# Prompt attention with both key heads side by side: scores in two PSUM banks at once, value products alternating between column halves

## The chip, the core and the metric

The kernel runs on one core of one Trainium2 chip. The metric is the device time of one execution in microseconds (us), a median of three runs. A profile of one more execution lists what each engine did: PE is TensorE (PEld its weight loads), DVE VectorE, ACT ScalarE, POOL GpSimd, SP the queue that issues most DMAs.

## What is computed

One inference step of a hybrid decoder with two layers, for a prompt of 512 tokens and for 8 sample sequences of 8 tokens that share the weights. Each layer has a token-mixing half (attention, convolution, retention and gated DeltaNet from one input projection, merged with gates) and a channel-mixing half. The change lies in the attention of the token-mixing half: 4 query heads in 2 groups over 2 key heads of 64 channels. For each block of 128 prompt queries, with the causal mask in the bias:

```
s = jnp.einsum('bqkgd,bnkd->bkgqn', qb, kb[:, :, 0]).astype(jnp.float32) + jnp.transpose(rb[t5_bucket(dist)], (2, 3, 0, 1))
p = masked_softmax(s, mask)
return jnp.einsum('bkgqn,bnkd->bqkgd', p.astype(dt), kb[:, :, 1])
...
o = g[:, :, 0] * o_c + g[:, :, 1] * o_s + g[:, :, 2] * o_w
```

There are three branches: compressed blocks (`o_c`), selected blocks (`o_s`, at this length all of them) and the sliding window (`o_w`). The sample sequences also need scores of their 8 query rows against 2048 cached keys, which lie in pages of the cache.

## The kernel before

The program is traced in Python and put in order by a list scheduler with its own estimates of time. What runs on the chip is a fixed order per engine; each engine works through its own and waits on semaphores. Pools give out tiles: a tag with `bufs=n` has n slots, and a new tile of that tag waits until the old one in its slot has been read.

`nsa` runs `nsa_prompt` and `sample_scores` in turns, a piece of the one and a piece of the other. Beside them the scheduler puts the products of the merges (`mm`, lines 335 to 337: 128x288 in fp32r, three per 128 channels), which depend on neither and serve as filling for PE; those that find no place here follow later. All other products here are plain fp32, and each is two PE instructions in the trace.

`nsa_prompt` first makes the compressed keys and values and that branch's probabilities, then goes over 4 query blocks i (with i+1 key blocks of 128 each), 2 groups g, 2 key heads kv and 2 branches br (selected, window). One unit (i, g, kv, br) is a chain over four engines:

- PE, L1551: scores of 128 queries against n = i+1 key blocks, contraction over 64 channels (rows 0-63 or 64-127 of the array, by the key head), into one bank of tag `s`.
- DVE L1553 adds the bias, L1555 takes the negated maximum; ACT L1557 makes the exponentials `E` with their sum; DVE L1558 and L1560 divide and apply the gate.
- PE L1563 transposes E by blocks into the single bank `t`; ACT (the helper on L603) copies it to `ET`.
- PE L1567: n value products into 64 of the 128 partitions of bank `o`, by the key head. L1546 puts the product of the compressed branch there before.

`sample_scores` loads pages by indirect DMAs on POOL (L1421, two of 128 KB for each `pg` tile, 8 tiles in all) and multiplies them on PE (L1590). One of its 8 units per layer takes 4 `pg` tiles, so that the other 4 can be loading. Its results lie in one bank of `s` and in bank `ax` of another pool; after every second unit ACT copies both out.

PSUM has 8 banks: 3 for `mm`, 1 for `ax`, and in this phase 2 for `s`, 1 for `t`, 1 for `o`.

## Time and profile before

| | us |
|---|---|
| median of 3 runs | 2760.32 |
| the runs | 2750.40, 2761.28, 2760.32 |
| span of the profiled execution | 2759.1 |
| stretch of the prompt attention, layer 0 (577 to 733 us) | 156 |
| the same, layer 1 (1934 to 2090 us) | 156 |

The span is what the profile shows of one execution, from the first to the last instruction; the page gives no other time of that execution. PE is busy for 94% of the span. The two stretches begin at the first score product of a layer and end with the last products on the sample's cached keys.

### The profile page before, as it was taken

The numbers are of one execution on the slowest core, as the hardware profiler recorded it, in microseconds if no ns is written. First come the engines' busy times: TensorE is split into PE (matmuls) and PEld (weight loads), VectorE is DVE, ScalarE is ACT, GpSimd is POOL, SyncE is SP. The second block draws the span as 40 slices with busy tenths as digits, with TensorE's granted clock in tenths as the row PEclk, the third lists the DMA queues.
The fourth block names the chain that finished last, engine by engine and source line by source line (L and its number), as shares of the span: only waits on it lengthen the run. The fifth ranks groups of instructions, "written<-read, shape, count | busy, mean of one in ns | idle before, by whom it ended". The sixth has DMA issues, their size and how long they took to land. (4 is left out here: it accounts for less than half of the span.)

```text
span 2759.1 us, 54028 instructions
## 1 busy us (share of the span) xinstructions
PE 2600.8 (94%) x22658; PEld 2275.4 (82%) x22658; DVE 1412.4 (51%) x2892; ACT 933.2 (34%) x1777; POOL 635.0 (23%) x827
## 2 busy tenths in 40 slices
PE   6999999988989999999989999999889999999998
PEld 4768777866779999999987687788657899999997
DVE  5878533333534573435578784432336155634455
ACT  4315112322323453323452342222233244433233
POOL 2102321223352320101122022212334333101012
PEclk9999989998999999999999999989799999999999
DMA  8643344322353242332466324413224451423324
GB/s 304 208 171 119 131 139 177 108 88 70 112 161 100 95 130 85 128 101 84 127 217 225 117 92 136 151 55 123 62 77 147 126 168 42 125 84 127 101 81 133
DMA packets 125058, 346.74 MB, mean 126 GB/s; under 512 B 28076, under 2 KB 47536, under 8 KB 118608
## 3 DMA queue, kind: packets, MB, share of 16 engines
q1 hardware_dynamic: 104016, 275.05, 30.6%
q0 software_dynamic: 20800, 68.25, 7.9%
q8 instruction: 178, 2.92, 0.4%
q14 instruction: 64, 0.52, 0.1%
HBM read 330.77 MB, written 20.73 MB: 127 GB/s over the span
## 5 line engine op out<-in xcount | busy, mean ns | idle before, releaser
L335 PE MATMUL mm<-hh,whi 128*128 128x288 f32 x3136 | 959.4, 306 | 8.8 <-ACT whi L287 4.1
L337 PE MATMUL mm<-hh,wlo 128*128 128x288 f32 x3136 | 948.8, 303 | 5.7 <-DVE wlo L288 4.2
L336 PE MATMUL mm<-hl,whi 128*128 128x288 f32 x3136 | 951.5, 304 | 2.5 <-issue 2.5
L288 DVE TENSOR_TENSOR wlo<-raw,whi 128x1024 fp32r<-128x1024 f32 (+1 forms) x320 | 391.6, 1226 | 577.5 <-ACT whi L287 538.3
L335 PEld LDWEIGHTS mm<-hh,whi 128*128 128x128 f32 x3136 | 602.8, 192 | 40.5 <-issue 22.7
L336 PEld LDWEIGHTS mm<-hl,whi 128*128 128x128 f32 x3136 | 606.2, 193 | 24.5 <-issue 20.9
L337 PEld LDWEIGHTS mm<-hh,wlo 128*128 128x128 f32 x3136 | 603.3, 192 | 23.2 <-issue 15.1
L287 ACT ACTIVATE whi<-raw 128x1024 fp32r<-128x1024 f32 (+1 forms) x320 | 334.9, 1048 | 562.0 <-PE mm L336 328.4
L337 PE MATMUL mm<-acth,wlo 128*128 128x288 f32 x704 | 206.4, 295 | 2.0 <-DVE wlo L288 2.0
L335 PE MATMUL mm<-acth,whi 128*128 128x288 f32 x704 | 208.2, 296 | 0.1
L336 PE MATMUL mm<-actl,whi 128*128 128x288 f32 x704 | 207.7, 296 | 0.0
L558 POOL COPY nfp<-gb 128x2 f32<-128x2 f32 x44 | 42.4, 964 | 611.8 <-ACT gb L532 611.8
L1421 POOL DMA_INDIRECT pg<-ck,ix x128 | 125.8, 983 | 183.6 <-PE sc L1590 89.5
L1786 POOL TENSOR_TENSOR f<-f,gate 128x288 f32<-128x288 f32 x80 | 77.1, 974 | 319.3 <-DVE gate L1785 316.2
L337 PEld LDWEIGHTS mm<-acth,wlo 128*128 128x128 f32 x704 | 131.9, 188 | 2.6 <-DVE wlo L288 2.5
L336 PEld LDWEIGHTS mm<-actl,whi 128*128 128x128 f32 x704 | 132.9, 189 | 0.8 <-DVE actl L344 0.5
L335 PEld LDWEIGHTS mm<-acth,whi 128*128 128x128 f32 x704 | 132.2, 188 | 1.2 <-ACT acth L343 1.0
L1421 POOL DMA_INDIRECT fil<-cc,ix x64 | 69.1, 1079 | 178.6 <-PE cmps L1462 165.0
L697 DVE SCALAR_TENSOR_TENSOR cvy<-cgb,par,cvy 128x512 f32<-128x512 f32 x120 | 91.8, 782 | 0.0
L1785 DVE SCALAR_TENSOR_TENSOR gate<-gate,mm 128x288 f32<-128x288 f32 x80 | 35.8, 450 | 101.6 <-PE mm L337 92.4
L1764 ACT ACTIVATE gate<-mm 128x288 f32<-128x288 f32 x112 | 45.2, 403 | 122.4 <-PE mm L337 103.4
L1553 DVE TENSOR_TENSOR s<-s,nb 128x256 f32<-128x256 f32 (+1 forms) x64 | 25.5, 398 | 118.4 <-PE s L1551 96.0
(585 smaller groups left out, 4262.0 us busy)
## 6 DMA issues: line engine op xcount, KB each, us to landing
raw<-wtr SPq DMA_DIRECT2D x124, 512.0 KB
raw<-wup SPq DMA_DIRECT2D x104, 512.0 KB
f<-wada SPq DMA_DIRECT2D x32, 1024.0 KB
fil<-wada SPq DMA_DIRECT2D x16, 1024.0 KB
raw<-wdn SPq DMA_DIRECT2D x32, 512.0 KB
raw<-wdn SPq DMA_DIRECT2D x32, 448.0 KB
raw<-wbr SPq DMA_DIRECT2D x16, 512.0 KB
raw<-wout SPq DMA_DIRECT2D x16, 512.0 KB
```

The lines of the kernel that those rows point to most:

```text
L287: nc.scalar.activation(hi, raw, AF.Copy)
L288: nc.vector.tensor_sub(lo, raw, hi.bitcast(F32))
L335: nc.tensor.matmul(ps, hi[:, k0 + k], ah[:, s], start=first, stop=False)
L336: nc.tensor.matmul(ps, hi[:, k0 + k], al[:, s], start=False, stop=False)
L337: nc.tensor.matmul(ps, lo[:, k0 + k], ah[:, s], start=False, stop=last)
L558: nc.gpsimd.tensor_copy(newp[:, ft], g[:, SEQ:SEQ + 2])
L697: nc.vector.scalar_tensor_tensor(y[:, :SEQ], gb[:, j:j + SEQ], wj(j), y[:, :SEQ], op0=OP.mult, op1=OP.add)
L1421: self.nc.gpsimd.indirect_dma_start(out=dst, out_offset=None, in_=self.ap[src], in_offset=bass.IndirectOffsetOnAxis(ap=ix[:, l, b, j:j + 1 ...
L1553: nc.vector.tensor_add(S[:, lo:], S[:, lo:], nb[:, hd, (0 if i else P):])
L1764: self.nc.scalar.activation(gts[hf], ps, AF.Tanh, scale=0.5)
L1785: nc.vector.scalar_tensor_tensor(gm, gm, 1.0, ps, op0=OP.add, op1=OP.mult)
L1786: nc.gpsimd.tensor_add(fm, fm, gm)
```

## The change

The loop over key heads moves inside the loop over branches. For each (i, g, br):

- one tile `s2` of two banks (a single slot) replaces the two slots of `s`; the scores of both key heads are written one behind the other, each into its own bank and from its own half of the array's rows;
- the steps on DVE and ACT are the same, for one head after the other; both `E` and both `ET` slots are taken by the two heads of one pair;
- the value products of the two heads alternate, block by block, between partitions 0-63 and 64-127 of `o`. A new helper, `in_one_go`, keeps all of them behind the first, which needs the `ET` that is ready last;
- the two products of the compressed branch stand side by side.

`sample_scores` takes two units at once: 8 `pg` tiles (16 indirect DMAs) are loaded, then all products run in one go, those on the last loaded tiles first. Its results, and the few products at the start of `nsa_prompt`, use bank `t` in place of `s`. The rest of the diff takes out comments and docstrings.

```diff
+    @contextmanager
+    def in_one_go(self):
+
+        info = mybir.DependencyInfo(mybir.DependencyClass.NoSync, mybir.DependencyReason.SCHED_ONLY)
+        ins = self.nc.cur_bb.bb.instructions
+        n = len(ins)
+        yield
+        first, *rest = [i for i in self.nc.cur_bb.bb.instructions[n:] if isinstance(i, mybir.InstMatmult)]
+        for i in rest:
+            self.tc.add_manual_dep(i, first.name, info, reason="in one go")
...
-        ps = self.ps("s", 2)
+        ps = self.ps("t")
...
+        rows = [slice(64 * kv, 64 * kv + 64) for kv in range(2)]
         for i in range(4):
             s = slice(i * P, (i + 1) * P)
             nk = (i + 1) * P
+            lo = max(0, i - 1) * P
             for g in range(2):
                 po = self.ps("o")
-                for kv in range(2):
-                    b = 64 * kv
+                for kv, r in enumerate(rows):
                     hd = 2 * kv + g
-                    nc.tensor.matmul(po[b:b + 64, :P], vc[32 * hd:32 * hd + 32, b:b + 64], PcT[32 * hd:32 * hd + 32, s],
-                                     start=True, stop=False, tile_position=(32 * hd, b))
-                    for br in range(2):
-                        ps = self.ps("s", 2)
-                        S = ps[:, :nk]
-                        nc.tensor.matmul(S, q[g][b:b + 64, s], kT[br][b:b + 64, :nk], start=True, stop=True)
-                        lo = max(0, i - 1) * P
-                        nc.vector.tensor_add(S[:, lo:], S[:, lo:], nb[:, hd, (0 if i else P):])
+                    nc.tensor.matmul(po[r, :P], vc[32 * hd:32 * hd + 32, r], PcT[32 * hd:32 * hd + 32, s],
+                                     start=True, stop=False, tile_position=(32 * hd, 64 * kv))
+                for br in range(2):
+                    S = self.cps.tile([P, 2, 512], F32, tag="s2", name="s2", bufs=1)
+                    for kv, r in enumerate(rows):
+                        nc.tensor.matmul(S[:, kv, :nk], q[g][r, s], kT[br][r, :nk], start=True, stop=True)
+                    E = []
+                    for kv in range(2):
+                        hd = 2 * kv + g
+                        nc.vector.tensor_add(S[:, kv, lo:nk], S[:, kv, lo:nk], nb[:, hd, (0 if i else P):])
                         nm, ss = self.pt("nm", (1,), bufs=4), self.pt("ss", (1,), bufs=4)
-                        nc.vector.tensor_reduce(nm, S, AX.X, OP.max, negate=True)
-                        E = self.pt("E", (SEQ,), bufs=2)
-                        nc.scalar.activation(E[:, :nk], S, AF.Exp, bias=nm, accum_out=ss)
+                        nc.vector.tensor_reduce(nm, S[:, kv, :nk], AX.X, OP.max, negate=True)
+                        e = self.pt("E", (SEQ,), bufs=2)
+                        nc.scalar.activation(e[:, :nk], S[:, kv, :nk], AF.Exp, bias=nm, accum_out=ss)
                         nc.vector.reciprocal(ss, ss)
                         gc = gt[:, i, 4 * (br + 1) + hd:4 * (br + 1) + hd + 1]
-                        nc.vector.tensor_scalar(E[:, :nk], E[:, :nk], ss, gc, op0=OP.mult, op1=OP.mult)
+                        nc.vector.tensor_scalar(e[:, :nk], e[:, :nk], ss, gc, op0=OP.mult, op1=OP.mult)
+                        E.append(e)
+                    ET = []
+                    for kv in range(2):
                         pt = self.ps("t")
                         for j in range(i + 1):
-                            nc.tensor.transpose(pt[:, j * P:(j + 1) * P], E[:, j * P:(j + 1) * P], self.ident)
-                        ET = self.pt("ET", (SEQ,), bufs=2)
-                        self.evac(ET[:, :nk], pt[:, :nk])
+                            nc.tensor.transpose(pt[:, j * P:(j + 1) * P], E[kv][:, j * P:(j + 1) * P], self.ident)
+                        et = self.pt("ET", (SEQ,), bufs=2)
+                        self.evac(et[:, :nk], pt[:, :nk])
+                        ET.append(et)
+                    with self.in_one_go():
                         for j in range(i + 1):
-                            nc.tensor.matmul(po[b:b + 64, :P], kvb[j][:, P * br + b:P * br + b + 64], ET[:, j * P:(j + 1) * P],
-                                             start=False, stop=br == 1 and j == i)
+                            for kv, r in reversed(list(enumerate(rows))):
+                                nc.tensor.matmul(po[r, :P], kvb[j][:, P * br + 64 * kv:P * br + 64 * kv + 64],
+                                                 ET[kv][:, j * P:(j + 1) * P], start=False, stop=br == 1 and j == i)
                 self.evac(o[g][:, s], po[:, :P])
                 yield
     def sample_scores(self, l, qd, Ss):
-        nc = self.nc
-        for G, i in ((0, 0), (0, 1), (0, 2), (0, 3), (1, 0), (1, 1), (1, 2), (1, 3)):
+        nc = self.nc
+        for G, i in ((0, 0), (0, 2), (1, 0), (1, 2)):
             big = []
-            for b4 in range(4):
-                pg = self.page_tile().rearrange("p (i a n) -> p i a n", i=2, a=2)
-                for t in range(2):
-                    self.pages(pg[:, t].rearrange("p a n -> p (a n)"), "ck", self.ix2, l, 4 * G + b4, 2 * i + t)
-                big.append(pg)
+            for u in range(2):
+                for b4 in range(4):
+                    pg = self.page_tile().rearrange("p (i a n) -> p i a n", i=2, a=2)
+                    for t in range(2):
+                        self.pages(pg[:, t].rearrange("p a n -> p (a n)"), "ck", self.ix2, l, 4 * G + b4, 2 * (i + u) + t)
+                    big.append(pg)
             yield
-            if i % 2 == 0:
-                sc = [self.ps("s", 2), self.ax("sc1")]
-            t = i % 2 * 2
-            with self.after_pe():
-                for kv in range(2):
-                    for b4 in range(4):
-                        for e in range(2):
-                            nc.tensor.matmul(sc[e][32 * b4:32 * b4 + 32, t * P:(t + 2) * P],
-                                             qd[64 * e:64 * e + 64, kv, 4 * G + b4].rearrange("p a g t -> p (a g t)"),
-                                             big[b4][64 * e:64 * e + 64, :, kv], start=kv == 0, stop=kv == 1,
-                                             tile_position=(64 * e, 32 * b4))
-            if t:
-                for e in range(2):
-                    self.evac(Ss[G][:, :PAST].rearrange("p (t e n) -> p t e n", e=2, n=P)[:, 2 * i - 2:2 * i + 2, e],
-                              sc[e].rearrange("p (t n) -> p t n", n=P))
+            yield
+            sc = [self.ps("t"), self.ax("sc1")]
+            with self.in_one_go():
+                for u in (1, 0):
+                    for kv in range(2):
+                        for b4 in (3, 2, 1, 0):
+                            for e in range(2):
+                                nc.tensor.matmul(sc[e][32 * b4:32 * b4 + 32, 2 * u * P:(2 * u + 2) * P],
+                                                 qd[64 * e:64 * e + 64, kv, 4 * G + b4].rearrange("p a g t -> p (a g t)"),
+                                                 big[4 * u + b4][64 * e:64 * e + 64, :, kv], start=kv == 0, stop=kv == 1,
+                                                 tile_position=(64 * e, 32 * b4))
+            for e in range(2):
+                self.evac(Ss[G][:, :PAST].rearrange("p (t e n) -> p t e n", e=2, n=P)[:, 2 * i:2 * i + 4, e],
+                          sc[e].rearrange("p (t n) -> p t n", n=P))
```

The number of instructions on each engine does not change (18413 on PE by the built program, where a product of two passes is one). Only their order does. Below, rows of the built order, without times; line numbers of the changed program are its own (L1564 scores, L1581 transposes, L1588 values, L1559 compressed branch, L1612 sample scores, L346 to L348 `mm`, L1432 page loads, L1807 the addition to `f`).

PE, second query block (i = 1), first group, layer 0. Before, each head's product stands alone:

```order
L1546 MATMUL o<-PcT,vc 64x128
L1551 MATMUL s<-kwin,nq 128x256
L1563 MATMUL t<-cst,E 128x128 x2
L1551 MATMUL s<-ksel,nq 128x256
L337 MATMUL mm<-bh,wlo 128x288
L1567 MATMUL o<-ET,kvb_6066 64x128
L1567 MATMUL o<-ET,kvb_6094 64x128
L335 MATMUL mm<-bh,whi 128x288
```

The same place now:

```order
L1559 MATMUL o<-PcT,vc 64x128 x2
L1581 MATMUL t<-cst,E 128x128 x2
L1564 MATMUL s_6505<-kwin,nq 128x256 x2
L1581 MATMUL t<-cst,E 128x128 x2
L346 MATMUL mm<-hh,whi 128x288
L347 MATMUL mm<-hl,whi 128x288
L348 MATMUL mm<-hh,wlo 128x288
L346 MATMUL mm<-hh,whi 128x288
L1588 MATMUL o<-ET,kvb_6066 64x128 x2
L1588 MATMUL o<-ET,kvb_6094 64x128 x2
```

Scores, values and compressed products of the two heads now stand in twos. This holds for all 16 value groups and all 8 compressed pairs of a layer, and for 10 of the 16 score pairs. In the other 6, all with i = 2 or 3, the scheduler puts the transposes of the pair before between the two scores.

PE, third query block (i = 2), layer 0, before:

```order
L1551 MATMUL s<-kwin,nq 128x384
L337 MATMUL mm<-hh,wlo 128x288
L335 MATMUL mm<-hh,whi 128x288
L1563 MATMUL t<-cst,E 128x128 x3
L336 MATMUL mm<-hl,whi 128x288
L337 MATMUL mm<-hh,wlo 128x288
L335 MATMUL mm<-hh,whi 128x288
L336 MATMUL mm<-hl,whi 128x288
L337 MATMUL mm<-hh,wlo 128x288
L1567 MATMUL o<-ET,kvb_6066 64x128
L1567 MATMUL o<-ET,kvb_6094 64x128
L1567 MATMUL o<-ET,kvb_6122 64x128
```

and now, at the same query block, a split pair:

```order
L1581 MATMUL t<-cst,E 128x128 x3
L1564 MATMUL s_6709<-kwin,nq 128x384
L1581 MATMUL t<-cst,E 128x128 x3
L1564 MATMUL s_6709<-kwin,nq 128x384
L1588 MATMUL o<-ET,kvb_6066 64x128 x2
L1588 MATMUL o<-ET,kvb_6094 64x128 x2
L1588 MATMUL o<-ET,kvb_6122 64x128 x2
```

There the second score of a pair moves behind the transposes of the pair before and directly ahead of that pair's values.

POOL, layer 0, from the start of the attention on, before (the row of 16 is two units of 8, and the second 8 wait for the products of a unit):

```order
L1530 MEMSET Pc 128x512
L1786 TENSOR_TENSOR f<-f,gate 128x288 x2
L1421 DMA pg<-ck,ix_158 128x256 x16
L1786 TENSOR_TENSOR f<-f,gate 128x288 x2
L1421 DMA pg<-ck,ix_158 128x256 x8
```

and now:

```order
L1541 MEMSET Pc 128x512
L1807 TENSOR_TENSOR f<-f,gate 128x288 x4
L1432 DMA pg<-ck,ix_158 128x256 x16
L1807 TENSOR_TENSOR f<-f,gate 128x288 x2
L1432 DMA pg<-ck,ix_158 128x256 x16
```

Page loads that were released 8 at a time are released 16 at a time, three times within the stretch where there were six releases.

## Rows read from the trace of the kernel before

**Rows 1.** The page: busy time, share of the span, instructions of each engine.

```profile
PE 2600.8 (94%) x22658; PEld 2275.4 (82%) x22658; DVE 1412.4 (51%) x2892; ACT 933.2 (34%) x1777; POOL 635.0 (23%) x827
```

**Rows 2.** Windows: length, busy us (instructions) by engine, granted clock, DMA share, GB/s.

```profile
577.00:733.00 156.00, 134.44 (x914) 95.38 (x914) 61.38 (x150) 49.32 (x130) 55.40 (x60) 0.88 0.23 70
...
1934.00:2090.00 156.00, 137.40 (x917) 96.20 (x916) 61.82 (x150) 49.65 (x131) 55.45 (x60) 0.87 0.23 70
```

**Rows 3.** Groups by form, 577 to 733: count | busy, mean ns | idle before.

```profile
L1567 PE MATMUL o<-ET,kvb 128*64 128x128 f32 x160 | 28.2, 314 | 16.5 <-ACT ET L603 13.2 <-issue 3.2
...
L1553 DVE TENSOR_TENSOR s<-s,nb 128x256 f32<-128x256 f32 x24 | 10.3, 431 | 47.8 <-PE s L1551 41.7 <-remote 3.1 <-PE o L1546 1.6
...
L1555 DVE TENSOR_REDUCE nm<-s 128x1 f32<-128x512 f32 x8 | 5.5, 690 | 0.2
L1557 ACT ACTIVATE E<-s,nm 128x512 f32<-128x512 f32 x8 | 5.5, 686 | 5.5 <-DVE nm L1555 5.5
```

**Rows 4.** Timeline of PE: start, duration in us, line, names, shapes, [idle before].

```profile
671.20 0.30 PE L335 MATMUL mm<-bh,whi 128*128 128x288 f32 x1
671.42 0.91 PE L1551 MATMUL s<-kwin,nq 64*128 64x384 f32 x2
672.26 0.55 PE L1563 MATMUL t<-cst,E 128*128 128x128 f32 x3
...
672.78 0.29 PE L337 MATMUL mm<-bh,wlo 128*128 128x288 f32 x1
...
673.18 0.29 PE L337 MATMUL mm<-bh,wlo 128*128 128x288 f32 x1
673.45 0.87 PE L1567 MATMUL o<-ET,kvb 128*64 128x128 f32 x6
674.25 0.40 PE L335 MATMUL mm<-bh,whi 128*128 128x288 f32 x1
674.49 0.30 PE L336 MATMUL mm<-bl,whi 128*128 128x288 f32 x1
```

**Rows 5.** Timeline of PE where two heads' scores happen to be neighbours.

```profile
695.18 0.69 PE L1551 MATMUL s<-kwin,nq 64*128 64x512 f32 x1
695.18 0.69 PE L1551 MATMUL s<-ksel,nq 64*128 64x512 f32 x1
...
696.24 1.09 PE L1567 MATMUL o<-ET,kvb 128*64 128x128 f32 x8
```

**Rows 6.** Timeline of PE from sample scores to compressed product to scores.

```profile
667.03 0.40 PE L1590 MATMUL s<-pg,qd 64*32 64x256 f32 x1
...
668.06 0.43 PE L1546 MATMUL o<-PcT,vc 32*64 32x128 f32 x2
668.41 0.59 PE L1551 MATMUL s<-ksel,nq 64*128 64x384 f32 x1
```

**Rows 7.** Timeline of PE in the sample's values: products on four column tiles.

```profile
791.21 1.06 PE L1731 MATMUL o<-pg,pT 128*32 128x128 f32 x26
792.20 0.49 PE L1728 MATMUL o<-nvx,cT 128*128 128x128 f32 x2
```

**Rows 8.** Timeline of PE around one of its long waits.

```profile
658.60 0.29 PE L336 MATMUL mm<-hl,whi 128*128 128x288 f32 x1
662.77 1.45 PE L1567 MATMUL o<-ET,kvb 128*64 128x128 f32 x6 [3.88 <-ACT ET L603]
```

**Rows 9.** Timeline of ACT at the same place.

```profile
662.23 0.49 ACT L603 ACTIVATE ET<-t 128x384 f32<-128x384 f32 x1 [3.94 <-remote]
```

**Rows 10.** Timeline of POOL, first and last of the 8 page loads there.

```profile
650.60 1.16 POOL L1421 DMA_INDIRECT pg<-ck,ix  x1 [3.45 <-PE sc L1590]
...
659.60 0.95 POOL L1421 DMA_INDIRECT pg<-ck,ix  x1 [0.30 <-issue]
```

**Rows 11.** Windows around the 14 page loads from 508 to 527, earlier in layer 0.

```profile
515.00:535.00 20.00, 16.79 (x87) 14.84 (x87) 4.38 (x16) 2.18 (x5) 9.18 (x11) 0.74 0.48 144
535.00:545.00 10.00, 10.00 (x86) 10.00 (x85) 1.33 (x2) 2.50 (x5) 0.00 (x0) 1.00 0.40 115
```

More of the change, by code (lines that the diff above doesn't have):

```diff
@@ L1488, in nsa_prompt @@
             nc.vector.tensor_scalar(kc[b:b + 64, b // 8:b // 8 + 8], ps[b:b + 64, :8], pc[b:b + 64], None, op0=OP.add)
-        ps = self.ps("s", 2)
+        ps = self.ps("t")
         for hd in range(4):
@@ L1507, in nsa_prompt @@
         Sc = self.pt("Sc", (4, 4, 8))
-        ps = self.ps("s", 2)
+        ps = self.ps("t")
         for g in range(2):
@@ L1512, in nsa_prompt @@
         self.evac(ST, ps[:64])
-        ps = self.ps("s", 2)
+        ps = self.ps("t")
         for i in range(4):
@@ L1531, in nsa_prompt @@
         nc.vector.tensor_mul(Pc[:, :, :, :8], Sc, b8(sm))
-        ps = self.ps("s", 2)
+        ps = self.ps("t")
         for i in range(4):
@@ L1540, in nsa_prompt @@
             nk = (i + 1) * P
+            lo = max(0, i - 1) * P
             for g in range(2):
                 po = self.ps("o")
-                for kv in range(2):
-                    b = 64 * kv
+                for kv, r in enumerate(rows):
                     hd = 2 * kv + g
-                    nc.tensor.matmul(po[b:b + 64, :P], vc[32 * hd:32 * hd + 32, b:b + 64], PcT[32 * hd:32 * hd + 32, s],
-                                     start=True, stop=False, tile_position=(32 * hd, b))
-                    for br in range(2):
-                        ps = self.ps("s", 2)
-                        S = ps[:, :nk]
-                        nc.tensor.matmul(S, q[g][b:b + 64, s], kT[br][b:b + 64, :nk], start=True, stop=True)
-                        lo = max(0, i - 1) * P
-                        nc.vector.tensor_add(S[:, lo:], S[:, lo:], nb[:, hd, (0 if i else P):])
+                    nc.tensor.matmul(po[r, :P], vc[32 * hd:32 * hd + 32, r], PcT[32 * hd:32 * hd + 32, s],
[8 more added lines that the diff above has]
+                        nc.vector.tensor_add(S[:, kv, lo:nk], S[:, kv, lo:nk], nb[:, hd, (0 if i else P):])
```

## Prediction

> **What bounds the kernel now.** First the page: PE is busy 94% of the span, far ahead of DVE and ACT [rows 1], so the end is set by PE's own order. Then the windows of the two stretches that the change touches: PE is busy 134.44 and 137.40 of 156 us, and the granted clock is 0.88 and 0.87 [rows 2]. A clock is either 2.4 or 1.2 GHz, so 0.88 means that about 0.24 of the stretch (37 us) ran at the lower level. Per layer the stretch holds some 20 us in which PE stands and some 18 to 20 us lost to the lower clock (0.12 x 156): 38 us that is not work at full clock.
>
> Third, who ends the waits. The groups put 16.5 us of PE's idle time before the value products, 13.2 of it on ACT's copy ET [rows 3]. Read alone that looks like the chain of a head. The timelines say otherwise. One such wait is 3.88 us [rows 8]; ACT's copy itself waited 3.94 us for something remote and began at 662.23 [rows 9]; and 8 page loads had been issued from 650.60 on, 1.26 us apart, the last at 659.60 [rows 10]. PE goes on about when the last page has landed (659.60 plus a landing of some 2.5). There are six such bursts of 8 in a stretch, and each is followed by a wait of 1.6 to 4.3 us and then by the lower clock. I put the 38 us down to them: 38/6 = **6.4 us per burst**. How loads hold up semaphores between PE and ACT the trace doesn't show, only that the two go together. An earlier burst of 14 loads fits: in 20 us around it PE ran 87 instructions, afterwards 86 in 10 us [rows 11], so it cost about 9.9 us.
>
> The filling products (`mm`) are as many as before; time saved in the stretch is saved in the end, since what finds no place there is done later at .13 us each in any case.
>
> **The change, part by part** (per layer; at full clock first).
>
> *Value products.* Two more products of a group lengthen it by 1.09 - .87 = .22 [rows 4, 5], so .11 us per instruction; 6 take .80 (673.45 to 674.25), so .14 is fixed. Ahead of the group stands .14 more than the .13 of an `mm` (673.18 to 673.45; three `mm` take .40 from 672.78), behind it .11 (674.25 to 674.49 is .24) [rows 4]. A separate group thus costs about .3 beyond its instructions. There are 160 value instructions in 32 groups. Does a product on columns 0-63 run beside one on 64-127? The nearest row is the sample's values on four column tiles with all rows: 26 in .99 us, .038 each [rows 7], against .11. So columns do overlap, and I take two at the price of one: 80 x .11 = -8.7. Sixteen groups fewer: 16 x .3 = -4.8. Sum **-13.5** (ends: -4.8 without overlap, -13.5 with all of it).
>
> A rule speaks against the first part. The Trainium skill, page "TensorE: Matmul & The Clock Gate", section "Part 3: Packing small matmuls — row/col tiling", says that weight loads overlap running matmuls only when the row group differs; here all rows are used by both. By it the 8.7 would not come, and it is a rival below. The .038 of [rows 7] speaks against it.
>
> *Scores.* One head at 384 keys takes .84 (671.42 to 672.26) [rows 4]. Where two heads happen to be neighbours, both at 512 keys start together and take 1.06 (695.18 to 696.24) [rows 5]: the second is nearly free, some .21 per key block. Ten of 16 pairs become neighbours (4 at i = 0, 4 at i = 1, 2 at i = 2 and 3): 4 x .21 + 4 x .42 + 2 x .75 = -4.0, less the two that were neighbours before (1.5) = -2.6. Eight groups fewer at about .35 are -2.8. Sum **-5.4**. The six split pairs give nothing; their second score now stands between transposes and values, which cover the wait for ET that `mm` covered before.
>
> *Compressed and sample products.* Two compressed products in a row take .35 for two instructions each way [rows 6]: eight entries fewer at .3 = -2.4. The sample's 32 instructions take 1.03 with their exit (667.03 to 668.06) [rows 6]; four groups fewer at .3 = -1.2. Sum **-3.6**.
>
> That is -22.5 at full clock. About a seventh of what PE does there runs at the lower one, which takes twice as long: **-25**.
>
> *New waits.* (a) One slot of `s2` in place of two of `s`: the next pair's scores wait for both exponentials. A head's steps are .43 + .69 on DVE and .69 on ACT at most [rows 3], so about 4.6 us for both heads; the longest pairs (i = 3) follow each other at some 10 us now (41 us for 4). No cost; if PE became twice as fast there, it would bind. (b) The sample's results in bank `t` must be copied out by ACT before the next transposes; a copy of 384 columns takes .49 [rows 9], so some .6 for 512, and the compressed products (.35) cover part: three times .4 = +1.2 (0 to 2). (c) All eight `pg` tiles are taken until the last sample scores, so the window pages behind them load later. From its issue a load took at most 3.2 us until PE went on (659.60 to 662.77) [rows 8, 10], and 36 `mm` (4.8 us) now stand ahead of the first use: +1 (0 to 4). (d) POOL does its four additions to `f` ahead of the first loads in place of two; it has the time.
>
> *The bursts.* Three of 16 in place of six of 8. Sixteen loads at 1.26 take 20.2 us, with the landing 22.5. Two bounds. Low: a burst costs the same whatever its length, 3 x 6.4 = 19. High: PE stands from about the sixth load until the last has landed (in [rows 10] it went on with its filling for some six loads), 16 us, and then runs 5 us longer for the clock: 3 x 21 = 63. Between them the burst of 14 scaled by its length: 9.9 x 16/14 = 11.3, 3 x 11.3 = 34 [rows 11]. This row is nearest in size, but its surroundings had more filling. I add 2 for the wait of the sample scores on pages between the first and second burst, where PE has only some 20 us of work, and take 36, against 38 now: **-2**. This is the term I know least.
>
> **Sum.** -25 + 1.2 + 1 - 2 = -25 per layer, -50 for both. The profiled span of 2759.1 becomes 2709; the median is 1.2 above that span, so **2710**.
>
> **Rivals.**
>
> 1. *Bursts cost by number, not by length*: the low bound, 19 in place of 36, 17 less per layer, about 2675. For it: the six waits look alike, and half of them would vanish. Against it: 9.9 for 14 loads [rows 11] is more than 6.4. Chance .15.
>
> 2. *Columns don't overlap* (the rule on weight loads): the 8.7, 10 with its seventh at half clock, is missing per layer: 2710 + 20 = 2730. Against it [rows 7], whose products are half as wide. Chance .10.
>
> 3. *Long bursts eat the gain*: what is saved elsewhere is 61 - 38 = 23 us per layer, so a burst of 16 that costs 61/3 = 20.5 us gives no change. That is close to the high bound: about 2764. PE would stand in each burst, since a chain that passes ACT must run for every block, and there are no more `mm` in the order to stand in for it. Chance .13.
>
> 4. *Slower: PE stands and then runs slow for half as long again*. The mechanism is the same, with PE stopped after the sixth load for 16.4 us and 8 us lost to the clock afterwards (3 to 4 us of waiting now bring about 3 us of loss): 24.6 per burst, 74 per layer in place of 38, +36 - 23 = +13, so 2759 + 26 = 2785. It decides above 20.5 us per burst. For it: PE's waits end with the last landing [rows 8 to 10], not with a fixed delay. Against it: 14 loads in a row did not do it. Chance .12.
>
> That the change does not do what it says is so for six of 16 score pairs, and is in the sum.
>
> **How the numbers follow.** The forecast has .50, with 2695 to 2735 as its own range (values -10 or +4, bursts 31 to 45 in place of 36). Left out of the range are half of rival 1 (2680 cuts it) and rival 4: **2680 to 2765**. A measurement of this kernel tells some 0.5%, 14 us, from no change: faster is below 2746, slower above 2774. Faster: .50 + .15 + .10 = .75; same: rival 3, .13; slower: rival 4, .12.
>
> **What would show it.** Value products: a group of 12 instructions (i = 2) should take some .8 from start to next start, as 6 do now; 1.46 says rival 2. Scores: neighbours start together, and a pair at 256 takes no longer than one. The windows of the stretch should be some 25 us shorter, with granted clock near 0.87 and PE idle near 18. Bursts: three, each followed by a wait; under 4 us each says rival 1, over 12 says 3 or 4. A wait of transposes on ACT behind the sample scores would be (b), one of the window's products on a load (c). DVE or ACT ending PE's waits outside the bursts, on `s2`, would show that the single slot binds, and that step (a) is wrong. The prediction falls if the 38 us do not belong to the page loads at all: then the windows keep their idle time wherever the loads stand.

## The result: 2778 us, slower by 0.7%, and the profile after

The changed kernel takes 2778.25 us (median of 15 runs), the kernel before 2760.01 beside it: a ratio of 1.0069 with a 95% interval of 1.0047 to 1.0092. The forecast was 2710, with 2680 to 2765. The profiled execution has a span of 2777.2 against 2759.1.

One thing has to be known for what follows: in some sessions on the chips the kernel before took about 2755, as in the profile ahead of the prediction, in others about 2635, once of each kind on a chip of the same number; every ratio below is taken within one session, and each experiment says which kind it met.

PE did do its work in less time. The page of the changed kernel, busy time (share), for [rows 1]:

```profile
PE 2571.8 (93%) x22658; PEld 2261.6 (81%) x22658; DVE 1402.1 (50%) x2892; ACT 932.1 (34%) x1777; POOL 632.8 (23%) x827
```

That is 29 us less busy and 47 us more idle. Where, is seen when stretches with the same work are compared: from one and the same weight split ahead of the attention to the last product of the sample scores, and from there to a weight split behind the sample's values, for each layer. Windows of the kernel before (length; busy us and instructions of PE, PEld, DVE, ACT, POOL; granted clock; DMA share; GB/s), layer 0, layer 1, then the two stretches behind:

```profile
530.00:732.70 202.70, 180.94 (x1275) 138.88 (x1273) 71.72 (x171) 60.33 (x151) 55.92 (x61) 0.90 0.26 79
1849.00:2089.00 240.00, 216.93 (x1514) 170.10 (x1512) 88.69 (x210) 73.83 (x173) 70.36 (x76) 0.90 0.28 85
...
732.70:988.70 256.00, 242.14 (x1970) 220.02 (x1971) 121.31 (x206) 97.02 (x190) 91.85 (x97) 0.99 0.39 123
2089.00:2228.00 139.00, 129.84 (x1094) 112.06 (x1087) 55.67 (x97) 40.16 (x74) 57.67 (x55) 0.99 0.46 142
```

The same four of the changed kernel:

```profile
526.40:731.00 204.60, 169.56 (x1272) 133.47 (x1271) 65.65 (x169) 59.55 (x150) 56.88 (x61) 0.81 0.24 73
1850.00:2091.00 241.00, 200.56 (x1518) 162.80 (x1516) 82.44 (x208) 73.50 (x175) 71.55 (x76) 0.85 0.26 81
...
731.00:991.00 260.00, 241.67 (x1986) 219.25 (x1971) 122.23 (x208) 97.03 (x190) 92.99 (x97) 0.99 0.39 125
2091.00:2244.00 153.00, 136.42 (x1085) 117.21 (x1084) 56.81 (x98) 40.33 (x74) 56.65 (x54) 0.93 0.43 134
```

In the first stretch of layer 0 PE's busy time falls by 11.4 although the granted clock falls from 0.90 to 0.81; with busy time at the lower level halved it is 21.4 us less work (20.2 in layer 1). But PE stands 35.0 us in place of 21.8 (40.4 in place of 23.1 in layer 1), and its work takes 28.0 us longer for the lower clock in place of 18.0 (26.0 in place of 22.2). That is less than the granted clock times the length suggests (0.19 x 204.6 = 39), since PE stands during part of the low time, and that part must not be counted twice. Gain and loss cancel: -21.4 + 13.3 + 10.0 = 1.9 (204.6 for 202.7), and 241 for 240. Behind it 4 and 14 us are added. With some 4 us less ahead of the first stretch, these make up the 18 us.

What stops PE is seen at the first burst of 16 page loads of layer 0. PE of the changed kernel (start, duration, line, names, shapes, idle before):

```profile
594.92 0.38 PE L1612 MATMUL sc<-pg,qd 64*32 64x256 f32 x1
595.22 0.43 PE L1559 MATMUL o<-PcT,vc 32*64 32x128 f32 x4
601.00 0.69 PE L1581 MATMUL t<-cst,E 128*128 128x128 f32 x2 [5.34 <-issue]
601.62 1.23 PE L1564 MATMUL s<-kwin,nq 64*128 64x256 f32 x4
603.74 0.69 PE L1581 MATMUL t<-cst,E 128*128 128x128 f32 x2 [0.90 <-issue]
...
611.55 0.63 PE L1581 MATMUL t<-cst,E 128*128 128x128 f32 x2
...
618.01 0.69 PE L1581 MATMUL t<-cst,E 128*128 128x128 f32 x2 [4.29 <-ACT ET L614]
```

ACT over the same time:

```profile
600.35 0.60 ACT L614 ACTIVATE S<-t 128x512 f32<-128x512 f32 x1 [5.29 <-remote]
...
603.30 0.38 ACT L614 ACTIVATE ET<-t 128x256 f32<-128x256 f32 x1 [1.87 <-PE s L1564]
607.50 0.38 ACT L614 ACTIVATE ET<-t 128x256 f32<-128x256 f32 x1 [3.81 <-remote]
...
617.57 0.38 ACT L614 ACTIVATE ET<-t 128x256 f32<-128x256 f32 x1 [7.46 <-remote]
```

And POOL, the first and the last of the 16 loads:

```profile
594.60 0.97 POOL L1432 DMA_INDIRECT pg<-ck,ix  x1 [0.90 <-PE sc L1612]
...
613.47 0.95 POOL L1432 DMA_INDIRECT pg<-ck,ix  x1 [0.30 <-issue]
```

The last sample product ended at 595.30; ACT, which had nothing else to do, began to copy its results at 600.35. The transposes of 603.74 ended at 604.43 and were copied at 607.50, those of 611.55 ended at 612.18 and were copied at 617.57: hand-overs (from the end on PE to the start of the step that reads it) of 5.1, 3.1 and 5.4 us. Away from the loads the same hand-over takes 0.04 to 0.10 us. What ACT hands on is not late: the value products start 0.05 us after ACT's copy has ended. With the results in the single bank `t` the first of these waits stops every chain at once, since the next transposes need that bank.

### The profile page after: what moved, and what is told of

Same layout as the page of the kernel before. It is cut to its first block, busy times and chain, and to the rows that moved or that the text cites. A ratio compares the mean times of both kernels' runs of the same rounds, so it can differ in the third digit from the quotient of the medians.

```text
span 2777.2 us, 53987 instructions
## 1 busy us (share of the span) xinstructions
PE 2571.8 (93%) x22658; PEld 2261.6 (81%) x22658; DVE 1402.1 (50%) x2892; ACT 932.1 (34%) x1777; POOL 632.8 (23%) x827
## 3 DMA queue, kind: packets, MB, share of 16 engines
q0 software_dynamic: 20800, 68.25, 7.8%
## 5 line engine op out<-in xcount | busy, mean ns | idle before, releaser
L346 PE MATMUL mm<-hh,whi 128*128 128x288 f32 x3136 | 961.0, 307 | 11.8 <-issue 6.6
L348 PE MATMUL mm<-hh,wlo 128*128 128x288 f32 x3136 | 949.7, 303 | 8.5 <-issue 4.5
L346 PEld LDWEIGHTS mm<-hh,whi 128*128 128x128 f32 x3136 | 605.2, 193 | 47.6 <-issue 30.3
L348 PEld LDWEIGHTS mm<-hh,wlo 128*128 128x128 f32 x3136 | 605.3, 193 | 24.6 <-issue 17.3
L348 PE MATMUL mm<-acth,wlo 128*128 128x288 f32 x704 | 206.4, 295 | 2.1 <-DVE wlo L299 2.1
L346 PE MATMUL mm<-acth,whi 128*128 128x288 f32 x704 | 208.1, 296 | 0.1
L1807 POOL TENSOR_TENSOR f<-f,gate 128x288 f32<-128x288 f32 x80 | 79.9, 1007 | 368.8 <-DVE gate L1806 362.4
L1432 POOL DMA_INDIRECT pg<-ck,ix x128 | 125.1, 977 | 127.0 <-issue 51.4
L348 PEld LDWEIGHTS mm<-acth,wlo 128*128 128x128 f32 x704 | 131.9, 188 | 2.7 <-DVE wlo L299 2.6
L346 PEld LDWEIGHTS mm<-acth,whi 128*128 128x128 f32 x704 | 132.1, 188 | 1.2 <-ACT acth L354 1.0
L1432 POOL DMA_INDIRECT fil<-cc,ix x64 | 68.8, 1075 | 172.0 <-PE cmps L1473 158.4
L346 PE MATMUL mm<-bh,whi 128*128 128x288 f32 x256 | 82.5, 325 | 8.6 <-ACT gate L1785 5.4
```

The source lines that it names most:

```text
L346: nc.tensor.matmul(ps, hi[:, k0 + k], ah[:, s], start=first, stop=False)
L348: nc.tensor.matmul(ps, lo[:, k0 + k], ah[:, s], start=False, stop=last)
L1432: self.nc.gpsimd.indirect_dma_start(out=dst, out_offset=None, in_=self.ap[src], in_offset=bass.IndirectOffsetOnAxis(ap=ix[:, l, b, j:j + 1 ...
L1807: nc.gpsimd.tensor_add(fm, fm, gm)
```

## The experiments

Each is told with the time of the kernel before in its session. Theory A: the indirect page loads hold up what PE hands on, and bursts of 16 do so more than twice as much as bursts of 8. Rival B: the new order itself makes the waits. Rival C: the bytes that land do.

**e1, e2, e9: the loads as plain ones.** The edit, in the changed kernel (e1, e9) and in the kernel before (e2); the order of every engine stays:

```diff
-self.pages(pg[:, t]..., "ck", self.ix2, l, 4 * G + b4, 2 * (i + u) + t)
+nc.gpsimd.dma_start(pg[:, t]..., self.ap["ck"][P * (2 * (i + u) + t):P * (2 * (i + u) + t) + P])
```

> The changed kernel with its page loads for the sample scores issued on POOL as plain DMAs of the same size (128 rows of 1 KB from a fixed place of the cache) in place of the indirect ones; the pages gathered are left out, so the sample's selected scores are those of other keys. The order of every engine is that of the changed kernel. Theory A (the indirect loads hold up what PE hands to ACT and DVE; in the changed kernel three bursts cost some 23 us each and layer): about 2778 - 2 x 65 = 2650, no PE wait over 2 us in the stretch. Theory B (the waits come from the new order itself: one slot of s2, results through bank t): 2770 to 2780, same waits. Theory C (the bytes that land, whoever issues them): 2770 to 2780 too, waits at the loads.

> The kernel before with the same replacement of the loads (the gather by page is left out). Theory A: its six bursts cost 38 us per layer, so about 2760 - 70 = 2690, some 45 above the changed kernel with plain loads. Theory B: the old order has no such waits of its own, so these are the loads' and it gains as in A, but the changed kernel does not. Theory C: 2760, no gain.

Both met a session in which the kernel before took 2635. e1: 2625.5, ratio 0.9974 (0.9960 to 0.9988). e2: 2634.8, ratio 1.0010 (0.9993 to 1.0026). None of the numbers expected came, since there the indirect loads cost the kernel before nothing (the same holds for e3 and e4 below, which met the same session). So the pair said nothing on A against C, but it raised another question: without any late hand-over the changed kernel gains 10 us, not the some 42 that PE saves.

> The changed kernel with plain loads again (the gather by page is left out), for a chip on which the kernel before takes about 2760. There, theory A: about 2640 to 2660, since the late hand-overs go with the indirect loads; theory C (bytes or completions of any load): 2765 to 2785. Where the kernel before takes 2635: 2620 to 2630 as it did.

Measured beside a kernel before of 2758.3: 2667.5, ratio 0.967 (0.958 to 0.976), 111 below the changed kernel on record, but 7 above the range of A: it is still 42 above e1, and 128 of the program's 256 indirect loads, in other stretches, were left as they are. ACT and POOL of e9 at the first burst:

```profile
587.10 0.60 ACT L614 ACTIVATE S<-t 128x512 f32<-128x512 f32 x1 [0.32 <-PE sc L1612]
```

```profile
586.34 8.46 POOL L1602 DMA_DIRECT2D pg<-ck  x16 [0.91 <-PE sc L1612]
```

The same 16 loads of the same size, issued on the same engine in 8.5 us in place of 20, and the copy of the sample's results waits 0.32 in place of 5.29. The stretch from the split to the last sample product:

```profile
517.80:671.10 153.30, 148.63 (x1290) 119.72 (x1288) 66.06 (x169) 59.90 (x151) 36.53 (x61) 0.98 0.32 99
1789.40:1972.00 182.60, 177.47 (x1515) 147.34 (x1513) 82.25 (x208) 73.59 (x173) 44.27 (x76) 0.98 0.35 106
```

51 and 58 us shorter than with indirect loads, with the same products in the same order. DMA packets and bytes of the whole program are the same in both profiles (20800 packets and 68.25 MB in POOL's queue). B and C fall as the cause of the long waits: it is the indirect form of the loads, not the order, the bytes or POOL as the issuing engine. The plain loads also read one fixed place in place of scattered pages; whether the addresses have a part was not tried apart.

**e5, e7: the changed kernel and the kernel before in a session of 2637.**

> The changed kernel once more, beside the kernel before. In the four runs so far the kernel before took 2635 and no hand-over from PE to ACT or DVE was late beside indirect page loads (0.04 us in the median, at most 0.4), while in the two recorded profiles it was 1.6 to 5.4 us late there. Theory A (the change loses only by these late hand-overs): where the kernel before takes about 2635, the changed kernel has none of them and takes what it took with plain loads, 2620 to 2628; where the kernel before takes about 2760, it takes 2775 to 2785. Theory B (the new order itself loses): 0.7% above the kernel before in either case.

> The kernel before itself, for its profile on this chip: where it takes about 2635, hand-overs from PE beside page loads of 0.04 to 0.1 us and two stretches of about 121 us; where it takes about 2760, late ones of 1.4 to 4 us and two stretches of 156 us (theory A). Theory B has the same hand-overs in both.

e5: 2625.3, ratio 0.9961 (0.9939 to 0.9983); e7: 2643.3, one run. Windows of e7 (stretch of layer 0, what is behind it, and the same of layer 1):

```profile
502.70:671.30 168.60, 166.96 (x1288) 128.86 (x1287) 71.96 (x171) 60.05 (x150) 61.17 (x66) 1.00 0.32 100
671.30:926.50 255.20, 243.66 (x1974) 222.11 (x1975) 122.24 (x207) 97.23 (x191) 91.89 (x97) 0.97 0.39 124
1772.00:1970.00 198.00, 196.26 (x1516) 157.04 (x1514) 88.57 (x210) 73.84 (x173) 71.70 (x76) 1.00 0.34 103
1970.00:2108.90 138.90, 131.16 (x1090) 113.97 (x1088) 55.95 (x96) 40.28 (x74) 56.15 (x54) 0.98 0.46 141
```

and of e5:

```profile
501.70:653.30 151.60, 146.10 (x1290) 117.92 (x1288) 67.41 (x169) 59.87 (x150) 63.23 (x67) 1.00 0.34 105
653.30:914.10 260.80, 244.89 (x1978) 221.91 (x1976) 123.26 (x210) 97.40 (x191) 92.28 (x97) 0.98 0.40 125
1760.40:1943.00 182.60, 176.82 (x1516) 147.06 (x1514) 84.07 (x208) 73.48 (x173) 75.11 (x76) 0.99 0.34 106
1943.00:2091.40 148.40, 133.32 (x1087) 114.91 (x1088) 56.66 (x98) 40.84 (x74) 57.76 (x54) 0.97 0.45 139
```

Here the kernel before stands 1.6 us in its stretch in place of 21.8, with all hand-overs at 0.04 to 0.1 us beside indirect loads. Its stretches are 34 and 42 us shorter than on record. So the 38 us per layer of the prediction were the loads', as it said, and they are gone in a session in which the loads don't hold PE up. The change then gains 17.0 and 15.4 us in the stretches and gives back 5.6 and 9.5 behind them. The changed kernel's stretches are 53 and 58 us shorter than on record. Theory A holds: the sign of the change turns with the late hand-overs.

**e3, e10: the prompt part alone, bursts of 8.** The sample's scores one unit at a time, 8 loads and 16 products, copied out at once:

```diff
-for G, i in ((0, 0), (0, 2), (1, 0), (1, 2)):
+for G, i in ((0, 0), (0, 1), (0, 2), (0, 3), (1, 0), (1, 1), (1, 2), (1, 3)):
...
-    self.evac(Ss[G]...[:, 2 * i:2 * i + 4, e], ...)
+    self.evac(Ss[G]...[:, 2 * i:2 * i + 2, e], ...)
```

> The prompt part of the change alone: pairs of heads as in the changed kernel, but the sample's scores one unit at a time again (bursts of 8 loads, 16 products in a row), each unit's results through bank t and copied out at once. Theory A: the gain on PE (22 us at full clock per layer) stands and the bursts cost what they did: 2705 to 2720. Theory B: the waits belong to the pairs, so 2765 to 2785.

> The prompt part alone, with bursts of 8, again. Where the kernel before takes about 2760, theory A: bursts of 8 cost what they did and the gain on PE stands, 2700 to 2725; if the cost follows the number of loads and not the length of a burst, 2745 to 2765. Where the kernel before takes 2635: 2612 to 2620 as it did.

e3 (before 2635.0): 2615.5, ratio 0.9932 (0.9906 to 0.9958). e10 (before 2758.3): 2729.3, ratio 0.990 (0.982 to 0.998). The pairs gain in both sessions; e10 is 4 above the range of A and far below that of the other theory. The windows of e10, which hold 32 and 43 PE instructions fewer than those of the changed kernel:

```profile
527.10:708.40 181.30, 158.53 (x1240) 119.32 (x1238) 66.42 (x168) 58.96 (x155) 56.65 (x60) 0.89 0.29 89
1830.00:2040.20 210.20, 187.59 (x1475) 147.76 (x1473) 84.59 (x207) 72.28 (x178) 72.65 (x75) 0.91 0.32 98
```

PE stands 22.8 us in layer 0, the granted clock is 0.89: about what it was with bursts of 8 before the change.

**e4, e15: the sample part alone, bursts of 16, heads one by one as before.**

`nsa_prompt` is that of the kernel before, `sample_scores` that of the changed one:

```diff
-for G, i in ((0, 0), (0, 1), (0, 2), (0, 3), (1, 0), (1, 1), (1, 2), (1, 3)):
+for G, i in ((0, 0), (0, 2), (1, 0), (1, 2)):
...
-sc = [self.ps("s", 2), self.ax("sc1")]
+sc = [self.ps("t"), self.ax("sc1")]
```

> The sample part of the change alone: heads one by one as before, but 16 loads and 32 products in a row as in the changed kernel, results through bank t. Theory A: 30 to 35 us per layer more in waits and low clock, no gain on PE: 2815 to 2835. Theory B: 2755 to 2770.

> Old heads with bursts of 16 again: where the kernel before takes 2760, the bursts' 30 to 35 us per layer come on top of the 21 that it lost where the kernel before takes 2635: 2830 to 2860. Where it takes 2635: 2656 as it did.

e4 (before 2635.0): 2655.9, ratio 1.009 (1.005 to 1.013). e15 (before 2752.8): 2861.3, ratio 1.039 (1.034 to 1.044). This part alone costs 21 us where hand-overs are prompt and 108 where they are late (1 above the range expected). So some loss is the order's own, whatever the hand-overs do. ACT of e15 in its second burst (loads from 641.26 to 660.11):

```profile
662.71 0.49 ACT L614 ACTIVATE ET<-t 128x384 f32<-128x384 f32 x1 [11.73 <-remote]
```

**e11, e13: pairs with bursts of 4.** Half units: two `pg` tiles, 4 loads, 8 products, 16 times a layer; `nsa_prompt` gives way after each branch, so that the two stay in step.

```diff
-for G, i in ((0, 0), (0, 2), (1, 0), (1, 2)):
+for G, i, h in [(G, i, h) for G in range(2) for i in range(4) for h in range(2)]:
...
-    for b4 in range(4):
+    for b4 in (2 * h, 2 * h + 1):
```

> The prompt part of the change with the sample's scores in half units: two pg tiles, so 4 loads and 8 products in a row, 16 times per layer, results copied out for 64 partitions each time. Theory A (a hand-over is late when several indirect loads are already under way; the first four of a burst were harmless in the recorded profile of the kernel before): where the kernel before takes about 2760 the waits beside loads nearly vanish, 2680 to 2705; where it takes 2635, 2610 to 2625 as with bursts of 8. Rival D (each load costs the same wherever it stands): where the kernel before takes 2760, 2725 to 2760 as with bursts of 8 or more, since the loads are as many.

> Pairs with bursts of 4 again, for a chip on which the kernel before takes about 2760, where the expectation of e11 was not tried: 2680 to 2705 if short bursts are harmless, 2725 to 2760 if each load costs the same. Where it takes 2635: 2629 as it did.

e11 (before 2635.6): 2629.4, ratio 0.9985 (0.9964 to 1.0007), no difference and 4 above the range of A. e13 (before 2752.8): 2704.8, ratio 0.982 (0.977 to 0.987), in the range of A and, in such a session, the lowest of the kernels that gather the pages as they should. Its windows:

```profile
528.20:697.00 168.80, 153.21 (x1231) 113.92 (x1229) 65.86 (x167) 63.93 (x171) 55.82 (x60) 0.96 0.32 96
1821.20:2017.80 196.60, 181.60 (x1467) 142.34 (x1465) 82.43 (x206) 77.53 (x194) 71.45 (x75) 0.99 0.34 105
```

The loads are as many as in e10, but 15.6 and 15.0 us of standing and a clock of 0.96 and 0.99 replace 22.8, 22.6 and 0.89, 0.91. The new place to give way is no gain in itself: without late hand-overs e11 takes 14 us more than e3. The length of a burst sets its cost, not the number of loads (rival D of e11) and not the number of bursts (the first rival of the prediction). In layer 0 the first four bursts of e13 come in twos without a gap, and there a hand-over is late up to 11.7 us after the first load, as with bursts of 8.

**e12, e14: half as many loads of twice the row.**

```diff
-for t in range(2):
-    self.pages(pg[:, t]..., "ck", self.ix2, l, 4 * G + b4, 2 * (i + u) + t)
+self.pages(pg..., "cv", self.ix4, l, 4 * G + b4, i + u)
```

> The changed kernel with 8 indirect loads of 128 rows of 2 KB (another table, so the sample's selected scores are those of other data) in place of 16 of 1 KB: the same bytes, half the loads and rows. Where the kernel before takes 2760: if the number of loads or rows sets the hold-up, about half of the 70 us per layer goes, 2695 to 2725; if the bytes do, 2765 to 2785. Where it takes 2635: 2615 to 2628.

> Half as many indirect loads of twice the row (other data) again, same condition: 2695 to 2725 if the number of loads or rows sets the hold-up, 2765 to 2785 if the bytes do. Where the kernel before takes 2635: 2627 as it did.

e12 (before 2635.6): 2627.4, ratio 0.9969 (0.9941 to 0.9996), like e5. e14 (before 2752.8): 2712.8, ratio 0.985 (0.979 to 0.991), 65 below the changed kernel on record with the same bytes, in the range expected for loads or rows. The number of loads (or rows) in a burst counts, the bytes don't.

**e6: the loads spaced** by an addition of 128 x 320 on POOL, kept behind each load and ahead of the next. It was meant to bring them 2.4 us apart; with additions of 0.8 us in the mean they came 1.9 apart.

```diff
 self.pages(...)
+nc.gpsimd.tensor_add(gap, gap, gap)
```

> The changed kernel with one addition of 128 x 320 on a scratch tile on POOL behind every page load of the sample scores (about 1.1 us), so that the loads come about 2.4 us apart in place of 1.26; PE's order stays. Theory A, with late hand-overs present: the loads no longer pile up, each burst's waits shrink, 2720 to 2750; if the delay belongs to each load however they are spaced, 2770 to 2800, since the loads then lie beside PE for twice as long. With no late hand-overs on the chip: within 5 us of the changed kernel.

Measured beside 2637.4: 2662.2, ratio 1.010 (1.007 to 1.013). That is 37 above e5, not within 5: 16 loads now take 29 to 30 us, and the sample's products waited 10.0 us for a page at 606.2, a wait that the text had not thought of. Whether spaced loads would help where hand-overs are late was not tried.

**e8: the value products of a pair, one head after the other.**

```diff
-for j in range(i + 1):
-    for kv, r in reversed(list(enumerate(rows))):
+for kv, r in reversed(list(enumerate(rows))):
+    for j in range(i + 1):
```

> The changed kernel with the value products of a pair still in one go, but first all of one head and then all of the other; only their order on PE differs. In the recorded profile of the changed kernel the 160 value instructions of a layer take 10.8 us at full clock, before 21.6. Theory A (columns overlap): they go to about 16 (21.6 less the entries saved, 16 x .3), so 5 to 6 us more per layer, 8 to 12 in all. Theory B (the saving is the grouping alone): within 3 us of the changed kernel.

e8 (before 2758.3): 2787.8, ratio 1.011 (1.003 to 1.019), 10 us more than the changed kernel in another session, an interval too wide for a verdict between the two; their rows tell more. PE of the changed kernel at full clock, 12 and 16 value instructions and what follows:

```profile
676.23 0.88 PE L1588 MATMUL o<-ET,kvb 128*64 128x128 f32 x12
677.03 0.40 PE L346 MATMUL mm<-hh,whi 128*128 128x288 f32 x1
...
721.34 1.09 PE L1588 MATMUL o<-ET,kvb 128*64 128x128 f32 x16
722.37 0.40 PE L348 MATMUL mm<-hh,wlo 128*128 128x288 f32 x1
```

and of e8:

```profile
710.31 1.63 PE L1588 MATMUL o<-ET,kvb 128*64 128x128 f32 x16
711.87 0.40 PE L347 MATMUL mm<-hl,whi 128*128 128x288 f32 x1
```

Sixteen take 1.03 in turns and 1.56 head by head (medians at full clock 1.02 and 1.51; for 12, 0.81 and 1.07). Eight, four of each head, take 0.59 either way: columns overlap there without alternating. Summed by these medians, the 16 groups of a layer take 14.2 in place of 11.1: 3 us more per layer, where theory A expected 5 to 6 and theory B none. Most of the saving needs the two heads in one group, not their alternation.

## Why the prediction was wrong, step by step

**What bounds the kernel.** Right: the 38 us per layer that PE stood or ran slow belonged to the page loads and not to the head's chain. e9 takes the indirect loads away and the waits go; e7 shows the kernel before without late hand-overs, 1.6 us of standing. The 9.9 us of [rows 11] were the loads' too: beside the same 14 loads PE of e7 runs 160 instructions in 20 us at a granted 1.00, in place of 87 at 0.74. The landing, put at 2.5 us, has a median of 2.8 in e7.

**Value products.** The mechanism was right: 12 instructions take 0.80 as 6 did [rows 4], and all 160 of a layer 10.8 us at full clock in place of 21.6. That is -10.8 inside the groups, close to 8.7 and .14 for each of 16 groups. The rest of the .3 per group lies in its neighbours, the `mm` (62.0 to 58.3 us in layer 0), where it can't be told from what the scores' groups save; so the -13.5 may still hold. The rule of the Trainium skill's page "TensorE: Matmul & The Clock Gate" ("Part 3: Packing small matmuls — row/col tiling"), by which weight loads on the same rows would not overlap, is not borne out: a group of 12 would have taken 1.46.

**Scores, compressed, sample products.** -4.2, -2.8 and -0.6 in layer 0 against -5.4, -2.4 and -1.2. Two heads' scores at 384 keys take what one takes (e5, start to next start 0.85 for four instructions). With the 3.7 of the `mm`, the work of PE fell by 21.4 and 20.2 us per layer at full clock, against 22.5 forecast.

**New waits.** (a) The single slot of `s2` was priced at nothing and costs 3.5 us per layer on record, behind late chains, and 1.4 in layer 0 of e5: three groups by form of the changed kernel, 561 to 731 us (count | busy, mean ns | idle before):

```profile
L1564 PE MATMUL s<-kwin,nq 64*128 64x512 f32 x8 | 5.5, 767 | 1.4 <-ACT E L1572 1.4
L1564 PE MATMUL s<-ksel,nq 64*128 64x384 f32 x8 | 5.1, 730 | 1.1 <-ACT E L1572 1.0
...
L1564 PE MATMUL s<-ksel,nq 64*128 64x512 f32 x8 | 4.3, 890 | 1.0 <-ACT E L1572 1.0
```

(b) The copy out of `t` was priced at 1.2 for its duration. The duration was not the point: the copy starts up to 5.1 us late. In e5, where nothing is late, PE's waits on it in layer 0 are 0.6 in all. (c) **The window pages, and what stands behind them, were mis-sized**: +1 (0 to 4) was forecast, 4 and 14 us came on record and 5.6 and 9.5 in e5. SP of the changed kernel, whose last sample product ended at 731.1:

```profile
735.23 1.86 SPq L1660 DMA_DIRECT2D pg<-kwin  x4
...
739.92 5.93 SPq L1660 DMA_DIRECT2D pg<-kwin  x4
```

and of the kernel before, where it ended at 732.7:

```profile
712.35 1.77 SPq L1639 DMA_DIRECT2D pg<-kwin  x4
...
737.25 1.79 SPq L1639 DMA_DIRECT2D pg<-kwin  x4
```

Half of them used to be on their way 20 us earlier. The 36 `mm` cover the first landing, but the sample's values, which need the same tiles after these pages, begin 34 and 36 us behind the last sample product in place of 29 (35 and 37 in e5; 27 in e3 and e10, where four window pages still load early). No wait of PE for a window page is over 0.3 us. What PE waits for instead in layer 1 is the sample's value pages (6.4 us in place of 2.1) and a gate from ACT ahead of an `mm` (3.6 in place of none); of the 14 us there, 7 are standing and 8 the lower clock, less 2 of work. So the text priced the first load, and what came is a later start of all that stands behind it. That the tiles held longer cause it is read from the order and these rows; no run moved the window pages alone. In e3 more of the gain stays than in e5 (0.9932 against 0.9961, intervals that overlap).

**The bursts: the step that failed.** Three of 16 were put at 36 us per layer, between 19 and 63, by scaling the burst of 14 of [rows 11]. Standing and lower clock together, from the result above, were 40 and 45 us in the two stretches before and are 63 and 66 now: 21 to 23 more per layer where 2 fewer were forecast. The text's own high bound, 63, is what came, a few us of (a) and (b) in it. Told by sessions, the stretches with late hand-overs are 34 and 42 us longer before and 53 and 58 now. Here the mechanism of rivals 3 and 4 came: in the stretch the long bursts took the whole gain, as in rival 3, and (c) put the time on the other side. Rival 4's time, 2785, was near; the chances, .13 and .12, were too low for a term that the text itself called the least known. The 14 loads were a poor measure. They ran beside `mm`, whose gaps the profile gives to no other engine, while here each block of a chain needs several hand-overs from PE, and many hand-overs during a burst took 1.4 to 6 us. And two things stood in the order: with 32 sample products in a row the first load goes out before they have ended, and their results lie in the only bank that the chains can use. The "first six loads" in which PE went on [rows 10] were a cover that the change took away.

**Range and chances.** 2765 as the upper end rested on the same 36; with the row of the high bound (63) and 4 more for the window pages the sum would have been 2772.

## What to carry to other kernels

A stall that comes with a burst of loads is priced by what must pass between engines during the burst, not by the burst's length times a row from another stage: ask which hand-over stands behind the first load, and what waits for that bank. Grouping products that release buffers also groups the loads that fill them; pairs of heads with bursts of 8 or 4 (e10, e13) were faster than both kernels where hand-overs are late; where they are prompt, bursts of 8 (e3) were the fastest and bursts of 4 (e11) no faster than the kernel before. The grouped loads without the pairs (e4, e15) were slower than either. When a buffer ring is held longer, price the whole chain of its next users, not the first load (here argued from rows, not shown by a run).

## What the runs showed of the hardware

- **PE's hand-overs beside indirect loads.** In the sessions of about 2755, ACT and DVE saw many of PE's results 1 to 6 us late beside indirect loads (up to 9.9 in e15), while ACT to DVE and ACT to PE stayed at 0.05 us. The latest came free 5.8 us after the first load of a burst of 4, 11.6 of 8, 23.0 of 16, and 11.5 for 8 loads with 2 KB rows: about 1.45 us per load, while the loads are issued every 1.26. Beside the 14 loads of [rows 11] PE ran 87 instructions in 20 us, against 160 in e7, with gaps of up to 0.8 us ahead of `mm` that the profile gives to no other engine; whether PE itself was held up there is not shown. Plain loads of the same size on POOL did nothing of the kind. What the loads and PE's signals share was not shown.
- **Two kinds of session.** The same programs met sessions in which none of this happened, and the kernel before was 120 us faster. On a chip of the same number, e5 to e7 met the one and e8 to e10 the other. Of the 16 completions of each load in the first burst of layer 0, the trace holds all in e7, 0 to 7 in the recorded profile of before, and all of the plain loads in e9. Every run has a recorded span and clock, so none tells whether the recording has a part in it. What makes the difference stays open, and with it, which sign the change has elsewhere: 1.0069 in the one, 0.9961 in the other.
- **Column halves.** Products on 64 of 128 columns, all rows in use, run two at a time: 12 instructions in 0.81, six in 0.80; with up to four of one head in a row they overlap even without alternating.
